# First head's stacks in three transfers by tokens, and values ahead of the spreading

## The chip, the cores and the metric

The kernel runs on one core of a Trainium2 chip. The metric is device time in microseconds, the median of several executions. One execution was also recorded by the hardware profiler; times inside it are counted from the start of its span. TensorE multiplies matrices, VectorE and ScalarE work elementwise, GpSimd does a few small operations, and SyncE issues every DMA of this kernel, in one queue.

## The reference

Two decoder layers over 1040 tokens (16 meta tokens and 1024 others) of width 1024, in float32. A layer computes

```
hn = rmsnorm(h, norm1_g)
q, k, v, u = split(hn @ w_in)
q, k = rope(q), rope(k)                       # 4 heads, two components of 64 each
lam = exp(sum(lam_q1*lam_k1)) - exp(sum(lam_q2*lam_k2)) + lam_init
a = softmax(q0 k0) - lam * softmax(q1 k1)     # causal
attn = rmsnorm(a @ v, subln_g) * (1 - lam_init)
conv = silu(layer_norm(depthwise(glu(u)), ...))
h = h + concat(attn, conv) @ w_out
h = h + (silu(gate) * up) @ w_down            # gate, up from rmsnorm(h, norm2_g)
```

and a last rmsnorm follows.

## The kernel before, in words

Activations lie transposed: channels on the 128 partitions, tokens along the rows. Each value that a matmul reads is split into a high and a low float32r part (`hh` and `hl` for the hidden state, two tiles for each weight), and a product takes three matmuls (high by high, high by low, low by high). Tokens are cut into three chunks, `CH0` = 0 to 272, 272 to 656, 656 to 1040.

The order on each engine is not that of the code. A scheduler of the tile framework simulates the program when it is built and fixes each engine's order and each tile's buffer. On the chip every engine then takes its own list strictly in turn. A row that waits holds up all behind it on its engine, and SyncE's list of DMAs is such a list. The DMAs count completion on eight semaphores in rotation, and a DMA that reuses one waits until the DMA eight places ahead has landed.

Layer 0 begins like this. While the input arrives, `project_qk` with `pre` multiplies the first two weight blocks of head 0 (accumulators `done`, L360): three chunks in PSUM tiles `pj` and three in `tr`. There are three `pj` buffers but only two `tr` buffers, so the third `tr` chunk (24 matmuls of 384 columns) needs one that has been copied out (L368). Beside it the squares of the hidden state are added up. `rsqrt_cols` sums them over the channels with one-column matmuls (L177) for nine blocks of tokens, VectorE scales (L179, L181), GpSimd takes the power -1/2 (L183). `spread` turns the nine columns into a row on all partitions: VectorE scales a diagonal (L198), TensorE multiplies by ones (L199), ScalarE copies out (L202). The tables of cosine and sine (L715) are multiplied by that row and used for the rope of q and k (L293), and the result is split into a pair of `ST` tiles (L285 on ScalarE for the high half, L286 on VectorE for the low half).

`make_stacks` then moves partitions with DMAs (L399): for each of the two components three tiles `S` of 128 rows, all from 32-row pieces of the `ST` pair. `small_params` loads the lambda parameters (L665) and reduces them to `nlam`. `project_v` makes the values chunk by chunk (L272, then ScalarE L428, a transpose L413 or L417, and ScalarE L414 or L420). `attention` takes query blocks of 16 and then eight times 128: `scores` (L455, L456, then VectorE and an exp on ScalarE, L466), the combination with `nlam` (L469 to L471), transposes (L483, L492) and values (L503). Between its steps the projection of the next head is woven in (`weave`). Weights come through `wsplit`: one DMA (L216), one ScalarE split (L222), one on VectorE (L223); `fetch` makes a block one ahead of the one asked for.

Of the kernel before, what the change touches and what calls it, by code (L numbers as in the profile page):

```python
# [10 lines left out]
F32 = mybir.dt.float32  # L11
F32R = mybir.dt.float32r
BF16 = mybir.dt.bfloat16
AF = mybir.ActivationFunctionType
# [5 lines left out]
L = 1040  # L20
D = 1024
KD = D // P
# [11 lines left out]
CH0 = ((0, 272), (272, 656), (656, 1040))  # L34
# [47 lines left out]
def tok(i):  # L82
    return (0, META) if i == 0 else (META + P * (i - 1), META + P * i)


def build(tc, xT, w_in, w_out, w_gu, w_down, params, lams, ctab, consts, tabs, outT):
    nc = tc.nc
    V, S, G, T_ = nc.vector, nc.scalar, nc.gpsimd, nc.tensor
# [12 lines left out]
    def nm(s):  # L101
        uid[0] += 1
        return f"{s}{uid[0]}"

    def big(dt=F32):
        return sp.tile([P, SW], dt, tag="S", name=nm("S"), bufs=SB)
# [11 lines left out]
    def tmp(dt=F32):  # L118
        return tp.tile([P, TW], dt, tag="T", name=nm("T"), bufs=TB)
# [15 lines left out]
    def small(n=NQ):  # L135
        return tp.tile([P, 16], F32, tag="small", name=nm("s"), bufs=16)

    def ps(tag):
        return pp.tile([P, 512], F32, tag=tag, name=nm(tag), bufs=PS_BUFS[tag])
# [29 lines left out]
    def rsqrt_cols(sq, n, blocks=range(NQ)):  # L169

        i0, i1 = blocks[0], blocks[-1] + 1
        pst = ps("sc")
        ms = small()
        V.memset(ms, 1.0)
        for i in blocks:
            a, b = tok(i)
            T_.matmul(pst[:b - a, i:i + 1], lhsT=sq[:, a:b], rhs=ones[:, 0:1], start=True, stop=True)  # L177
        f0 = max(i0, 1)
        V.tensor_scalar(ms[:, f0:i1], pst[:, f0:i1], 1.0 / n, EPS, op0=ALU.mult, op1=ALU.add)  # L179
        if i0 == 0:  # L180
            V.tensor_scalar(ms[:META, 0:1], pst[:META, 0:1], 1.0 / n, EPS, op0=ALU.mult, op1=ALU.add)  # L181
        rc = small()
        G.tensor_tensor(rc[:, i0:i1], ms[:, i0:i1], mhalf[:, i0:i1], op=ALU.pow)  # L183
        return rc

    def spread(rc, blocks=range(NQ), out=None):

        r = big() if out is None else out
        for k0, k1 in KCH:
            bl = [i for i in blocks if k0 <= tok(i)[0] < k1]  # L190
            if not bl:
                continue
            pb = ps("sc")
            dg = tmp()
            for i in bl:
                a, b = tok(i)
                n_ = b - a
                V.tensor_scalar(dg[:n_, a - k0:b - k0], ident[:n_, :n_], rc[:n_, i:i + 1], None, op0=ALU.mult)  # L198
                T_.matmul(pb[:, a - k0:b - k0], lhsT=ones[:n_, :], rhs=dg[:n_, a - k0:b - k0],  # L199
                          start=True, stop=True)  # L200
            lo, hi = tok(bl[0])[0], tok(bl[-1])[1]
            S.activation(r[:, lo:hi], pb[:, lo - k0:hi - k0], AF.Copy)  # L202
        return r
# [78 lines left out]
    hs = list(zip(hh, hl))  # L282

    def split(hi, lo, src):
        S.activation(hi, src, AF.Copy)  # L285
        V.tensor_tensor(lo, src, hi.bitcast(F32), op=ALU.subtract)  # L286
# [5 lines left out]
    def tt(o, a, b, op):  # L292
        V.tensor_tensor(o, a, b, op=op)  # L293
# [4 lines left out]
    def tick(c):  # L298

        credit[0] += c  # L300
        while credit[0] >= BGSTEP:
            credit[0] -= BGSTEP
            if bg:
                bg.pop(0)()
# [17 lines left out]
    def drain(*gens):  # L322
        for g in gens:
            for c in g:
                tick(c)
# [16 lines left out]
        return pads[which][turns[which] % 2]  # L342


    def project_qk(l, h, cosr, sinr, st, pre=None):
        if pre is None:
            wa = fetch("in", l, 3 * h)
            wb = fetch("in", l, 3 * h + 1)
        else:
            done = []  # L350
            for c0, c1 in CH0:
                done.append((ps("pj"), ps("tr")))
            lag = 2
            steps = [(i, k + lag * i) for i in range(2) for k in range(KD)]
            for i, k in sorted(steps, key=lambda t: (t[1], t[0])):
                k -= lag * i
                for q, (x, y) in enumerate(((0, 0), (0, 1), (1, 0))):
                    if True:
                        for c, (c0, c1) in enumerate(CH0):
                            T_.matmul(done[c][i][:, :c1 - c0], lhsT=pre[i][k][x],  # L360
                                      rhs=hs[k][y][:, c0:c1], start=(k == 0 and q == 0),
                                      stop=(k == KD - 1 and q == 2))
        st += [pair(F32R) for _ in range(2)]
        if pre is not None:
            ab = [big(), big()]
            for c, (c0, c1) in enumerate(CH0):
                for i in range(2):
                    S.activation(ab[i][:, c0:c1], done[c][i][:, :c1 - c0], AF.Copy)  # L368
        for c, (c0, c1) in enumerate(CH0):
            n = c1 - c0  # L370
            if pre is None:
                pa, pb = ps("pj"), ps("pj" if h else "tr")
                mm3(pa[:, :n], wa, hs, c0, c1)
            else:
                pa, pb = ab[0][:, c0:c1], ab[1][:, c0:c1]
            t = [tmp() for _ in range(4)]
            tt(t[0][:, :n], pa[:, :n], cosr[:, c0:c1], ALU.mult)
            tt(t[1][:, :n], pa[:, :n], sinr[:, c0:c1], ALU.mult)
            yield 10 * n
            if pre is None:  # L380
                mm3(pb[:, :n], wb, hs, c0, c1)
            tt(t[2][:, :n], pb[:, :n], sinr[:, c0:c1], ALU.mult)
            tt(t[3][:, :n], pb[:, :n], cosr[:, c0:c1], ALU.mult)
            tt(t[0][:, :n], t[0][:, :n], t[2][:, :n], ALU.subtract)
            tt(t[1][:, :n], t[1][:, :n], t[3][:, :n], ALU.add)
            for x in range(2):
                split(st[0][:, x, c0:c1], st[1][:, x, c0:c1], t[x][:, :n])
            yield 10 * n

    def make_stacks(st):  # L390
        stacks = []
        for c in range(2):
            q = slice(32 * c, 32 * c + 32)
            k = slice(64 + 32 * c, 96 + 32 * c)
            three = []
            for parts in (((0, q), (1, q)), ((0, k), (0, k)), ((1, k), (1, k))):
                s = big(F32R)
                for j, (x, rows) in enumerate(parts):
                    nc.sync.dma_start(s[64 * j:64 * j + 64, :L].bitcast(F32), st[x][rows].bitcast(F32))  # L399
                three.append(s)  # L400
            stacks.append(three)
        return stacks

    def project_v(l, h, rcol, out):
# [277 lines left out]
    for l in range(DEPTH):  # L682
# [9 lines left out]
        pre = None  # L692
        if l == 0:
            raws = []
            pre = []
            sqacc = big()
            for k in range(KD):
                if k in (0, 2):
                    pre.append(fetch("in", 0, k // 2))
                raw = big() if k else xraw  # L700
                raws.append(raw)
                if k:
                    nc.sync.dma_start(raw[:, :L], xT[k])
                gsplit(hh[k], hl[k], raw[:, :L], col("g1", 0, k))
                for c0, c1 in HALVES:
                    t = raw[:, c0:c1]
                    S.activation(sqacc[:, c0:c1] if k == 0 else t, t, AF.Square)
                    if k:
                        tt(sqacc[:, c0:c1], sqacc[:, c0:c1], t, ALU.add)
            nc.sync.dma_start(con, consts)  # L710
        rcol = rsqrt_cols(sqacc, D)
        rs = spread(rcol)
        cosr, sinr = big(), big()
        for t, i in ((cosr, 0), (sinr, 1)):
# [19 lines left out]
                if j in DVEJ:  # L734
                    conv_dve(l, j, zs[j][0], ys)

        st, vs = [], []
        drain(project_qk(l, 0, cosr, sinr, st, pre))
        if l == 0:
            for i in range(DEPTH):  # L740
                small_params(i)
        cats, fin = [], []
        for h in range(NH):
            stacks = make_stacks(st)
            vs = []
            drain(project_v(l, h, rcol, vs))
            if fin:
                finalize(*fin.pop())
            st = []
            if h + 2 == NH:  # L750
                fill, ratio = chain(project_qk(l, h + 1, cosr, sinr, st), glus((0,))), RA
            elif h + 1 < NH:
                fill, ratio = project_qk(l, h + 1, cosr, sinr, st), 1.3
            else:
                fill, ratio = glus((1, 2)), 1.8
            weave(attention(l, h, stacks, *vs, nlams[l], cats, fin), fill, ratio)
            drain(fill)
# [6 lines left out]
        for cat in cats:  # L764
            hi, lo = big(F32R), big(F32R)
            a = chunks[0][0]
# [118 lines left out]
        steps = [(j, q) for j in range(NF) for q in PRODS]  # L885
# [30 lines left out]
        for i, n in enumerate(OCN):  # L916
            w = fetch("oc", l, n)
            t = acc[n]
# [18 lines left out]
        for c, (s0, s1) in enumerate(sub):  # L937
            T_.matmul(sb[c][:, :s1 - s0], lhsT=xc["a11"][0][0][:, :P], rhs=xc["a11"][0][0][:, s0:s1],
                      start=True, stop=True)
# [67 lines left out]
        i = 0  # L1007
        for j in range(NF):
            gn = GROUPS[l][gi]
            m = len(mids)  # L1010
# [178 lines left out]
```

## Time and profile before

| | us |
|---|---|
| median of 3 runs (2387.89 to 2388.52) | 2388.34 |
| the profiled execution | 2387.03 |
| its span | 2385.3 |
| TensorE busy in the span | 2333.7 (98%) |
| VectorE busy | 1670.9 (70%) |
| ScalarE busy | 987.2 (41%) |

Busy time is an average over the whole span. The change concerns the first 80 us, and there the table of stretches tells more than the totals: busy time of each engine, the clock that TensorE was granted as a share of full speed, and what the DMA engines moved. The name behind an arrow in a row is what ended a wait.

### The profile page before, as it was taken

What the parts mean: (1) busy time and instruction counts of PE and PEld (TensorE: products, weight loads), DVE (VectorE), ACT (ScalarE), POOL (GpSimd) and SP (SyncE); (2) the same over time, 40 slices, a digit from 0 to 9 for tenths busy, and PEclk for the clock granted to TensorE, in tenths of its full rate; (3) what the DMA queues carried; (4) which work ended last, traced back from release to release, by engine and by line L of the source; (5) the groups of instructions that cost most, each with busy time, mean ns of one, the idle gap of its engine ahead of it and who ended that gap; (6) DMA issues with size and microseconds to landing.
All of it is one profiled execution on the core that took longest, in us unless ns stands there. A gap on an engine that the chain in (4) does not pass through costs nothing.

```text
span 2385.3 us, 36659 instructions
## 1 busy us (share of the span) xinstructions
PE 2333.7 (98%) x14407; PEld 2140.8 (90%) x14407; DVE 1670.9 (70%) x3476; ACT 987.2 (41%) x2074; POOL 33.8 (1%) x29
## 2 busy tenths in 40 slices
PE   8999999999999999999999999999999999999998
PEld 7899999989999999999999999987788888888887
DVE  7676799786656657566766768997856556556566
ACT  5565462553323223233535555536523223233242
POOL 0000000000000000000000000000000000000000
PEclk9999999999999999999999999999999999999999
DMA  4332422101112121111244314221121121111212
GB/s 163 94 76 68 121 66 61 49 29 60 46 45 64 35 63 40 59 56 43 90 128 102 74 44 112 76 54 45 36 62 55 43 62 39 59 59 39 60 56 71
DMA packets 84460, 155.29 MB, mean 65 GB/s; under 512 B 10048, under 2 KB 33600, under 8 KB 84288
## 3 DMA queue, kind: packets, MB, share of 16 engines
q1 hardware_dynamic: 84288, 152.95, 22.2%
q8 instruction: 114, 1.87, 0.3%
q14 instruction: 58, 0.48, 0.1%
HBM read 114.64 MB, written 8.45 MB: 52 GB/s over the span
## 4 chain that ended last, share of the span: by engine, by line
PE 86%; DVE 9%; ACT 2%; issue 1%; POOL 1%; DMA 1%; SPq 1%; DVEq 0%; POOLq 0%; ACTq 0%
PE pj L272 26%; PE sc L901 16%; PE pj L901 10%; PE tr L901 10%; PE sc L272 10%; DVE S L590 4%; PE tr L503 3%; PE tr L272 2%; PE sc L455 2%; PE tr L492 1%; PE sc L456 1%; PE sc L199 1%; DVE S L293 1%; DVE cw L610 1%; DVE S L286 1%
## 5 line engine op out<-in xcount | busy, mean ns | idle before, releaser
L272 PE MATMUL pj<-hh,w 128*128 128x384 f32 (+1 forms) x1776 | 342.5, 327 | 0.7 <-ACT S L368 0.7
L285 ACT ACTIVATE w<-w 128x512 fp32r<-128x512 f32 x308 | 187.0, 627 | 318.5 <-DVE w L293 242.9
L286 DVE TENSOR_TENSOR w<-w,w 128x512 fp32r<-128x512 f32 x308 | 209.5, 690 | 128.9 <-PE sc L901 53.8
L272 PE MATMUL pj<-S,w 128*128 128x384 f32 (+3 forms) x1164 | 296.2, 351 | 1.5 <-ACT S L285 0.9
L272 PEld LDWEIGHTS pj<-hh,w 128*128 128x128 f32 x1776 | 285.9, 189 | 2.7 <-ACT S L368 1.0
L901 PE MATMUL sc<-S,w 128*128 128x260 f32 (+1 forms) x1188 | 286.3, 322 | 0.0
L222 ACT ACTIVATE w<-w 128x512 fp32r<-128x512 f32 (+1 forms) x204 | 117.6, 577 | 308.3 <-DMA w<-in_w_down 167.9
L272 PEld LDWEIGHTS pj<-S,w 128*128 128x128 f32 x1164 | 204.4, 188 | 22.8 <-ACT S L285 1.9
L901 PEld LDWEIGHTS sc<-S,w 128*128 128x128 f32 x1188 | 198.6, 191 | 17.7
L272 PE MATMUL sc<-m,w 128*128 128x384 f32 (+3 forms) x804 | 211.5, 346 | 0.0
L272 PE MATMUL pj<-m,w 128*128 128x384 f32 (+3 forms) x804 | 211.4, 346 | 0.0
L901 PE MATMUL sc<-hh,w 128*128 128x260 f32 (+1 forms) x594 | 192.3, 324 | 6.9 <-ACT w L285 6.9
L901 PE MATMUL sc<-hl,w 128*128 128x260 f32 (+1 forms) x594 | 190.9, 321 | 0.0
L272 PE MATMUL pj<-hl,w 128*128 128x384 f32 (+1 forms) x888 | 174.4, 327 | 0.0
L223 DVE TENSOR_TENSOR w<-w,w 128x512 fp32r<-128x512 f32 (+1 forms) x204 | 127.1, 623 | 51.7 <-ACT w L222 45.2
L901 PE MATMUL tr<-S,w 128*128 128x260 f32 (+1 forms) x594 | 157.8, 320 | 3.1 <-ACT S L802 3.1
L901 PE MATMUL tr<-hl,w 128*128 128x260 f32 (+1 forms) x594 | 158.1, 320 | 0.0
L901 PE MATMUL pj<-S,w 128*128 128x260 f32 (+1 forms) x594 | 158.1, 320 | 0.0
L901 PE MATMUL pj<-hh,w 128*128 128x260 f32 (+1 forms) x594 | 157.7, 320 | 0.0
L272 PEld LDWEIGHTS sc<-m,w 128*128 128x128 f32 x804 | 143.1, 188 | 12.7
L272 PEld LDWEIGHTS pj<-m,w 128*128 128x128 f32 x804 | 143.1, 188 | 12.6
L590 DVE SCALAR_TENSOR_TENSOR S<-S,par,S 128x1037 f32<-128x1037 f32 (+15 forms) x120 | 153.2, 1278 | 0.6
(214 smaller groups left out, 4599.4 us busy)
## 6 DMA issues: line engine op xcount, KB each, us to landing
w<-in_w_gu SPq DMA_DIRECT2D x176, 256.0 KB, 3.0
S<-ST SPq DMA_DIRECT2D x96, 260.0 KB, 5.2
w<-in_w_in SPq DMA_DIRECT2D x80, 256.0 KB, 3.2
w<-in_w_down SPq DMA_DIRECT2D x96, 192.0 KB, 2.4
w<-in_w_out SPq DMA_DIRECT2D x32, 256.0 KB, 2.8
S<-in_xT SPq DMA_DIRECT2D x8, 520.0 KB, 7.3
w<-in_w_down SPq DMA_DIRECT2D x16, 256.0 KB, 2.7
S<-in_tabs SPq DMA_DIRECT2D x4, 520.0 KB, 5.4
```

Of the source, the lines that this page charges most:

```text
L199: T_.matmul(pb[:, a - k0:b - k0], lhsT=ones[:n_, :], rhs=dg[:n_, a - k0:b - k0], start=True, stop=True)
L222: S.activation(hi, rw, AF.Copy)
L223: V.tensor_tensor(lo, rw, hi.bitcast(F32), op=ALU.subtract)
L272: T_.matmul(out, lhsT=w[k][wi], rhs=xs[k][xi][:, c0:c1], start=(q == 0 and k == 0), stop=(q == 2 and k == n - 1))
L285: S.activation(hi, src, AF.Copy)
L286: V.tensor_tensor(lo, src, hi.bitcast(F32), op=ALU.subtract)
L293: V.tensor_tensor(o, a, b, op=op)
L455: T_.matmul(pc[:sz, :n], lhsT=qs[:, qa:qb], rhs=kk[:, k0:k1], start=True, stop=False)
L456: T_.matmul(pc[:sz, :n], lhsT=qs[:, qa:qb], rhs=kl[:, k0:k1], start=False, stop=True)
L503: T_.matmul(po[:sz, :P], lhsT=lh, rhs=rh, start=(j == 0), stop=(j == len(blocks) - 1))
L590: bg.append(lambda o=o: V.scalar_tensor_tensor(y[:, o:L], z[:, :L - o], cw(o), y[:, o:L], op0=ALU.mult, op1=ALU.add))
L901: T_.matmul(outs[c][:, :s1 - s0], lhsT=w[wi][:, k * P:(k + 1) * P], rhs=xc[q][k][xi][:, s0:s1], start=(first and p == 0 and k == 0), stop= ...
```

## The change

It does two things, for layer 0 and head 0 only. The first q/k products are a function of their own, `first_qk`, called ahead of `rsqrt_cols`, and it copies its accumulators out at once; the values' generator is made there too, and its first stretch (the 272-token chunk) is run between `rsqrt_cols` and `spread`. And the stacks are moved chunk by chunk: `project_qk` calls `make_stacks` after each chunk's split, with the six stack tiles made beforehand. A part of a stack is moved by DMAs of 32 rows and 272 or 384 columns, 24 for a chunk, 72 in all, where twelve of 64 rows and 1040 columns did it. Later heads and layer 1 go as before.

```diff
-    def project_qk(l, h, cosr, sinr, st, pre=None):
-        if pre is None:
+    def first_qk(pre):
+
+        done = []
+        for c0, c1 in CH0:
+            done.append((ps("pj"), ps("tr")))
...
+        ab = [big(), big()]
+        for c, (c0, c1) in enumerate(CH0):
+            for i in range(2):
+                S.activation(ab[i][:, c0:c1], done[c][i][:, :c1 - c0], AF.Copy)
+        return ab
+
+    def project_qk(l, h, cosr, sinr, st, ab=None, stacks=None):
+        if ab is None:
             wa = fetch("in", l, 3 * h)
             wb = fetch("in", l, 3 * h + 1)
...
             for x in range(2):
                 split(st[0][:, x, c0:c1], st[1][:, x, c0:c1], t[x][:, :n])
+            if stacks is not None:
+                make_stacks(st, c0, c1, stacks)
             yield 10 * n
 
-    def make_stacks(st):
-        stacks = []
+    def make_stacks(st, c0=0, c1=L, into=None):
+        stacks = into or []
...
-            for parts in (((0, q), (1, q)), ((0, k), (0, k)), ((1, k), (1, k))):
-                s = big(F32R)
+            for m, parts in enumerate((((0, q), (1, q)), ((0, k), (0, k)), ((1, k), (1, k)))):
+                s = into[c][m] if into else big(F32R)
                 for j, (x, rows) in enumerate(parts):
-                    nc.sync.dma_start(s[64 * j:64 * j + 64, :L].bitcast(F32), st[x][rows].bitcast(F32))
+                    if into is None:
+                        nc.sync.dma_start(s[64 * j:64 * j + 64, :L].bitcast(F32), st[x][rows].bitcast(F32))
+                        continue
+                    for i in range(2):
+                        a = 64 * j + 32 * i
+                        nc.sync.dma_start(s[a:a + 32, c0:c1].bitcast(F32), st[x][rows, i, c0:c1].bitcast(F32))
...
+        ab, stacks, vs = None, None, []
+        if l == 0:
+            ab = first_qk(pre)
         rcol = rsqrt_cols(sqacc, D)
+        first_v = project_v(l, 0, rcol, vs)
+        if l == 0:
+            tick(next(first_v))
         rs = spread(rcol)
...
-        st, vs = [], []
-        drain(project_qk(l, 0, cosr, sinr, st, pre))
+        st = []
+        if l == 0:
+            stacks = [[big(F32R) for _ in range(3)] for _ in range(2)]
+        drain(project_qk(l, 0, cosr, sinr, st, ab, stacks))
         if l == 0:
             for i in range(DEPTH):
                 small_params(i)
...
-            stacks = make_stacks(st)
-            vs = []
-            drain(project_v(l, h, rcol, vs))
+            if l or h:
+                stacks = make_stacks(st)
+            if h:
+                vs = []
+                drain(project_v(l, h, rcol, vs))
+            else:
+                drain(first_v)
```

What the scheduler makes of it shows in two places. The first is TensorE's order around the norm's sums in layer 0. The changed kernel's lines are numbered differently: its L356 is L360 of before, and the tile `sc` written by L177 holds the sums. Before:

```order
L360 MATMUL tr_278<-hl_94,w_146 128x272
L360 MATMUL tr_280<-hl_94,w_146 128x384
L177 MATMUL sc_223<-ones,S_125 16x1
L177 MATMUL sc_223<-ones,S_125 128x1 x4
L360 MATMUL tr_278<-hh_86,w_147 128x272
L360 MATMUL tr_280<-hh_86,w_147 128x384
L177 MATMUL sc_223<-ones,S_125 128x1 x4
L199 MATMUL sc_240<-T_241,ones 128x16
```

And in the changed kernel, at the same place, where `tr_228` is the third chunk, of which the first and the last two of 24 matmuls are shown, and `pj_410` the first stretch of values:

```order
L177 MATMUL sc_381<-ones,S_125 16x1
L177 MATMUL sc_381<-ones,S_125 128x1 x4
L272 MATMUL pj_410<-hh_79,w_164 128x272
L272 MATMUL pj_410<-hh_80,w_164 128x272
L272 MATMUL pj_410<-hh_81,w_164 128x272
L356 MATMUL tr_228<-hh_79,w_140 128x384
...
L356 MATMUL tr_228<-hl_94,w_146 128x384
L356 MATMUL tr_228<-hh_86,w_147 128x384
L177 MATMUL sc_381<-ones,S_125 128x1 x4
L272 MATMUL pj_410<-hh_82,w_164 128x272
```

The last four blocks' sums now stand behind three matmuls of values and the 24 of the third chunk, and the rest of the first stretch of values follows them, ahead of the spreading.

The second place is SyncE's queue around the stacks of head 0 (`S` from `ST`). Before, from the lambda loads on:

```order
L665 DMA T_479<-in_lams 128x256
L665 DMA T_487<-in_lams 128x256
L216 DMA w_656<-in_w_in 128x512
L399 DMA S_495<-ST_427 64x1x1040
L399 DMA S_495<-ST_428 64x1x1040
L399 DMA S_498<-ST_427 64x1x1040 x2
L399 DMA S_501<-ST_428 64x1x1040 x2
L399 DMA S_504<-ST_427 64x1x1040
L399 DMA S_504<-ST_428 64x1x1040
L399 DMA S_507<-ST_427 64x1x1040 x2
L399 DMA S_510<-ST_428 64x1x1040 x2
L216 DMA w_662<-in_w_in 128x512
```

In the changed kernel, with the first and the last rows of the 72 transfers:

```order
L730 DMA S_465<-in_tabs 128x1040
L730 DMA S_466<-in_tabs 128x1040
L216 DMA w_722<-in_w_in 128x512
L407 DMA S_475<-ST_481 32x272 x2
L407 DMA S_475<-ST_482 32x272 x2
...
L407 DMA S_479<-ST_481 32x384 x4
L407 DMA S_480<-ST_482 32x384 x4
L674 DMA T_597<-in_lams 128x256
L674 DMA T_605<-in_lams 128x256
L216 DMA w_728<-in_w_in 128x512
```

The lambda loads moved from ahead of the stacks to behind all of them, and a weight block (`w_716`, `w_722`) moved ahead. On ScalarE the split of `w_728` stands ahead of the first query block's exps. On TensorE the first two scores of the fourth query block stand ahead of 24 matmuls of the next head's projection, and the first block's transpose behind 20 of these.

## Rows read from the trace of the kernel before

**Rows 1.** Table of stretches, 25 to 95 us: busy time and instructions by engine, clock, DMA share, GB/s.

```profile
core 0: us, PE busy (x) PEld busy (x) DVE busy (x) ACT busy (x) POOL busy (x), PEclk, DMA share, GB/s
...
30.00:40.00 10.00, 6.76 (x39) 6.34 (x39) 4.45 (x17) 2.16 (x7) 1.80 (x1) 0.66 0.00 0
60.00:65.00 5.00, 4.53 (x28) 4.20 (x26) 0.32 (x2) 0.02 (x1) 0.00 (x0) 1.00 0.96 239
65.00:75.00 10.00, 5.65 (x25) 4.90 (x26) 3.12 (x19) 4.15 (x18) 0.00 (x0) 0.72 0.72 187
...
85.00:95.00 10.00, 10.00 (x68) 9.27 (x67) 8.86 (x34) 6.67 (x22) 0.00 (x0) 1.00 0.01 2
```

**Rows 2.** Waits of TensorE, 25 to 90 us: total, times, longest.

```profile
PE sc L199 <- DVE T L198: 2.5, 1, 2.5
PE sc L456 <- DMA S<-ST: 2.2, 1, 2.2
```

**Rows 3.** Instructions in order of time, SyncE's queue: start, duration, line, count.

```profile
49.78 2.16 SPq L665 DMA_DIRECT2D T<-in_lams  x2
...
52.63 13.17 SPq L399 DMA_DIRECT2D S<-ST  x12
65.90 3.61 SPq L216 DMA_DIRECT2D w<-in_w_in  x4
```

**Rows 4.** Instructions in order of time, all engines, 25 to 46 us.

```profile
30.95 0.95 PE L177 MATMUL sc<-ones,S 128*128 128x1 f32 x8
...
34.42 4.31 PE L199 MATMUL sc<-T,ones 16*128 16x16 f32 x18 [2.52 <-DVE T L198]
...
44.71 0.74 ACT L285 ACTIVATE ST<-T 128x272 fp32r<-128x272 f32 x2
45.16 0.79 DVE L286 TENSOR_TENSOR ST<-T,ST 128x272 fp32r<-128x272 f32 x2 [1.29 <-ACT ST L285]
```

**Rows 5.** The chain that ended last, in order of time, third chunk: start, duration.

```profile
40.10 4.20 PE tr L360 x24
```

**Rows 6.** One line's instructions, L199 in layer 1: durations in ns, first and last start.

```profile
L199 PE MATMUL sc<-T,ones x18: 257/275/278, 1217.8 to 1220.0; 128*128 128x128 f32 x16, 16*128 16x16 f32 x2
```

**Rows 7.** Instructions in order of time, SyncE's queue, start of the kernel and conv.

```profile
2.59 0.91 SPq L558 DMA_DIRECT2D ct<-in_ctab  x2
...
388.27 5.09 SPq L601 DMA_DIRECT2D S<-S  x8
```

**Rows 8.** DMA lines of SyncE: issue min/median/max in ns; landing of L601.

```profile
L601 SPq DMA_DIRECT2D S<-S x32: 571/597/1811, 352.0 to 1576.6; - x32
DMA to landing us min/median/max: 2.4/2.5/4.5
...
L399 SPq DMA_DIRECT2D S<-ST x12: 557/939/2090, 52.6 to 64.5; - x12
...
L216 SPq DMA_DIRECT2D w<-in_w_in x80: 327/328/2649, 1.6 to 1513.8; - x80
```

**Rows 9.** DMA issues by transfer: KB each, median us from issue to landing.

```profile
w<-in_w_in SPq DMA_DIRECT2D x80, 256.0 KB, 3.2
...
S<-in_tabs SPq DMA_DIRECT2D x4, 520.0 KB, 5.4
```

**Rows 10.** Instructions in order of time, all engines, 70 to 78 us, first query blocks.

```profile
70.46 0.49 PE L456 MATMUL sc<-S,S 128*16 128x16 f32 x2 [2.23 <-DMA S<-ST]
...
71.05 0.31 ACT L466 ACTIVATE p<-p,s 16x16 f32<-16x16 f32 x1 [3.65 <-DVE s L465]
...
71.36 0.61 ACT L222 ACTIVATE w<-w 128x512 fp32r<-128x512 f32 x1
...
72.61 0.22 DVE L471 SCALAR_TENSOR_TENSOR p<-p,s,p 16x16 f32<-16x16 f32 x1
...
74.34 0.19 PE L483 MATMUL tr<-con,p 16*16 16x16 f32 x1
...
77.61 0.27 PE L483 MATMUL tr<-con,p 128*16 128x128 f32 x1
```

More of the change, by code (lines that the diff above doesn't have):

```diff
@@ L342, in padded @@
         return pads[which][turns[which] % 2]
-    def project_qk(l, h, cosr, sinr, st, pre=None):
-        if pre is None:
+    def first_qk(pre):
+        done = []
+        for c0, c1 in CH0:
+            done.append((ps("pj"), ps("tr")))
+        lag = 2
+        steps = [(i, k + lag * i) for i in range(2) for k in range(KD)]
+        for i, k in sorted(steps, key=lambda t: (t[1], t[0])):
+            k -= lag * i
+            for q, (x, y) in enumerate(((0, 0), (0, 1), (1, 0))):
+                for c, (c0, c1) in enumerate(CH0):
+                    T_.matmul(done[c][i][:, :c1 - c0], lhsT=pre[i][k][x],
+                              rhs=hs[k][y][:, c0:c1], start=(k == 0 and q == 0),
+                              stop=(k == KD - 1 and q == 2))
+        ab = [big(), big()]
+        for c, (c0, c1) in enumerate(CH0):
+            for i in range(2):
[3 more added lines that the diff above has]
+        if ab is None:
             wa = fetch("in", l, 3 * h)
             wb = fetch("in", l, 3 * h + 1)
[L349 to L362, printed above, removed]
-        st += [pair(F32R) for _ in range(2)]
[L364 to L368, printed above, removed]
+        st += [pair(F32R) for _ in range(2)]
         for c, (c0, c1) in enumerate(CH0):
             n = c1 - c0
-            if pre is None:
+            if ab is None:
                 pa, pb = ps("pj"), ps("pj" if h else "tr")
@@ L379, in project_qk @@
             yield 10 * n
-            if pre is None:
+            if ab is None:
                 mm3(pb[:, :n], wb, hs, c0, c1)
@@ L395, in make_stacks @@
             three = []
-            for parts in (((0, q), (1, q)), ((0, k), (0, k)), ((1, k), (1, k))):
-                s = big(F32R)
+            for m, parts in enumerate((((0, q), (1, q)), ((0, k), (0, k)), ((1, k), (1, k)))):
+                s = into[c][m] if into else big(F32R)
                 for j, (x, rows) in enumerate(parts):
-                    nc.sync.dma_start(s[64 * j:64 * j + 64, :L].bitcast(F32), st[x][rows].bitcast(F32))
+                    if into is None:
[4 more added lines that the diff above has]
+                        nc.sync.dma_start(s[a:a + 32, c0:c1].bitcast(F32), st[x][rows, i, c0:c1].bitcast(F32))
                 three.append(s)
-            stacks.append(three)
+            if into is None:
+                stacks.append(three)
         return stacks
```

## The prediction

> **What bounds the kernel now.** I read the table of stretches first. TensorE is busy 10.00 of 10 us between 85 and 95 (and so it goes on), so a delay that reaches it there is not given back; it is idle for 3.24 us between 30 and 40 and for 4.35 us between 65 and 75, with a granted clock of 0.66 and 0.72 on average (its levels are 0.5 and 1.0 of full speed, 1.2 and 2.4 GHz) [rows 1]. Those two holes are all that the change can fill in this region: 7.6 us, and what the half clock costs. The waits of TensorE name the causes: 2.5 us for the spreading's VectorE scalings in the first hole, 2.2 us for the last stack transfers in the second [rows 2]. Then I followed SyncE's queue: two loads of lambda parameters from 49.78, twelve stack transfers that occupy the queue for 13.17 us from 52.63, weights behind them at 65.90 [rows 3].
>
> **The change part by part.** I place three events in the changed order and compare one position of TensorE: the transposes of the second query block, before at 77.61 [rows 10].
>
> *First hole.* The third q/k chunk (24 matmuls, 4.20 us [rows 5]) and the first stretch of values now stand ahead of the spreading. TensorE gets no more work. But the changed order also puts the last batch of the norm's sums (0.95 us, before from 30.95 to 31.90 [rows 4]) behind these 24 matmuls. They can start when ScalarE has copied the accumulator whose PSUM buffer they reuse; TensorE arrives there at about 31.05 by my estimate, since it saves the batch and gets three matmuls of values. 31.05 + 4.20 + 0.95 = 36.2: the pow on GpSimd, VectorE's scalings and all behind them start 4.3 us later than before. Something comes back: the spreading's 18 matmuls took from 34.42 to 38.73, 4.31 us, in the stretch of low clock [rows 1, 4]; in layer 1 the same 18 went from 1217.8 to about 1220.3, 2.5 us [rows 6]. That is 1.8, and the changed order takes some VectorE waiting out with it; I take 2.4 us later in all. The rope tables' loads stand behind a weight load that waits for the last matmul of the first two chunks, which stays near 29; with 5.4 us to land [rows 9] they arrive by 35 and are used near 41, so that move costs nothing, and each us beyond that slack would cost one.
>
> *First part of the stacks.* Before, the first chunk's high halves were written by 45.45 and the low ones by 45.95 [rows 4]. 2.4 us later, the first transfers (which need only the high halves) can go at about 47.6. Before, the first stack went at 52.63: 5.0 us are gained here.
>
> *The queue.* Twelve transfers become 72: 24 for each part, of 32 rows each. All 72 stand on SyncE ahead of both lambda loads, which before stood ahead of the stacks. The trace has no transfer of this shape. From below: plain loads from HBM take 0.327 us at least to issue [rows 8], with 0.05 between two 0.38; back to back they follow each other at 0.455 (two in 0.91 [rows 7]). From above: the conv's SBUF-to-SBUF transfers of 65 KB, eight in 5.09 us, 0.64 each [rows 7], of which the issue is 0.597, at least 0.571 [rows 8]. The old stacks took 0.557 at least, 0.939 in the median [rows 8]; the median is the engines' time for 260 KB, and the bytes in all are unchanged. I take 0.62, since the new ones are SBUF to SBUF too, as is each row with a least issue over 0.5. 72 x 0.62 = 44.6. The data are not late: the last chunk is split 2.4 us later than before, about 56, and is wanted at 47.6 + 48 x 0.62 = 77.
>
> By the Trainium skill (Perfetto Trace Analysis, section DMA Optimizations) splitting transfers may let some start sooner and so the whole end sooner, where the DMA engines are mostly idle. Here they moved 239 GB/s between 60 and 65 [rows 1], and what the split multiplies is the issue on one queue. The same skill (DMA: Bandwidth & Descriptors, section Issuing engines are not separate DMA queues) calls the time to initiate a DMA usually small beside the DMA itself. The conv's rows show 0.597 us of issue for 2.5 of landing [rows 8]; by the rule the queue would need little more than the bytes' 13.2 us, which is the third rival's case.
>
> *What waits for the queue.* The first query block needs lambda, now loaded at the queue's end: 47.6 + 44.6 = 92.2, and two plain issues (0.9) make 93.1. The weight load behind them counts as well, since the changed order puts its split on ScalarE ahead of the first block's exps: landing 3.2 [rows 9], split 0.61 [rows 10]. Before, from the second exp's start to the end of the subtraction it took 71.05 to 72.83 [rows 10]; now both exps lie there, 0.5 more, so 2.3. T = 93.1 + 3.2 + 0.6 + 2.3 = 99.2 for the first block's transpose, before at 74.34 [rows 10]. Lambda's own arithmetic hides beside that weight load. TensorE's order gives it nothing to do meanwhile: values, the next head's first projection chunk and 20 matmuls of its second run out by about 76, since the fourth block's first scores wait for 36 transfers: 47.6 + 22.3 + 2.5 = 72.4, later than the 70.46 at which scores resumed before [rows 10]. About 20 us of idle lie before that and 23 after it. The restart at a low clock I cost at nothing, since before had one too; it may cost 1.5 more.
>
> *The sum.* The second block's transpose came 3.27 us after the first [rows 10]; now T + 3.3 = 102.5. In the changed order 25 matmuls of 384 columns are still to do there that before were done: 25 x 0.175 (4.20 / 24) = 4.4. The delay is 102.5 + 4.4 - 77.6 = 29.3 us. From there both orders hold the same work and become the same within head 1, and TensorE stays full [rows 1]. The profiled execution took 2387.03 for a span of 2385.3; plus 29.3 that is 2416.3. The median of the runs shown is 1.3 above the profiled one, so I say 2417.
>
> **The rivals.** With y for one stack issue the delay is 72 y - 15.3.
>
> Second: the new transfers have plain patterns on both sides, so they cost what plain loads cost. For it: every row over 0.5 regroups partitions (64 or 128 rows from 32 or 16, or back), none of the new ones does. Against it: no SBUF-to-SBUF row is cheap. 0.455 gives +17.5, 2406; 0.38 gives +12.1, 2400.
>
> Third, the other side: the price goes with the rows. A quarter of the rows at a quarter of 0.327 is 0.08, with the gap 0.13, so the bytes decide, 13.2 us as before [rows 3]: 13.2 - 15.3 = -2.1 us, 2386. It decides below 0.21 an issue. Against it: in the program each transfer waits until the one eight places ahead has landed, and SBUF-to-SBUF landings take 2.4 at least [rows 8]; 2.4 / 8 = 0.30 would make it +6.3.
>
> Fourth: the queue costs what I say but half is given back, because the later blocks of head 0 find stacks, weights and lambda landed and TensorE's order waits less for VectorE. For it: VectorE was busy for only 3.12 of the ten us from 65 [rows 1]. Against it: TensorE is full after 85. 2403.
>
> That the first stretch of values doesn't fill the hole is no rival: it fills it, and the norm's chain is late for it.
>
> **How the numbers follow.** Forecast 0.64; plain price 0.18; price by rows 0.09; half given back 0.09. The likeliest gives 2417, its own range 2413 to 2423 (0.59 and 0.65 an issue, 1.5 us either way for the place of the first issue, the low clock). The range of eight in ten takes in half given back and the plain price at 0.455 and most of the way to 0.38: 2401 to 2423. About 0.2% (4.8 us) is what a measurement of this kernel can tell from no change. Slower by more: 0.64 + 0.18 + 0.09 = 0.91. The price by rows is split: same 0.06, and faster 0.03, if the holes close better than I reckon.
>
> **What would show it.** Right: SyncE issuing without a pause from about 47.6 until past 90, each stack transfer 0.55 to 0.62 us; the lambda loads behind; VectorE waiting for them longest of all it waits for early on; TensorE all but idle from about 76 to 99 at a low granted clock; the norm's last sums near 35 instead of 31. Wrong: issues below 0.25 us, lambda loads before 65, or TensorE busy in that stretch; then the second hole is closed and the kernel is no slower. If an issue costs 0.38 to 0.46, it is the price that fails, not the mechanism.

## The result, and the profile after

The changed kernel takes 2418.68 us (median of 4 runs, 2418.02 to 2419.91), the kernel before 2388.12 us on the same chip (4 runs). The ratio is 1.0129, with a 95% interval from 1.0117 to 1.0141: slower by 30.6 us, where 2417 had been forecast. The profiled execution took 2419.91 us for a span of 2418.1.

TensorE does no more work than before (14,407 matmuls, 2334.9 us busy against 2333.7). The table of stretches shows where it stands still; the columns are those of [rows 1].

```profile
30.00:40.00 10.00, 10.00 (x72) 9.70 (x71) 2.87 (x9) 3.15 (x8) 2.23 (x1) 1.00 0.45 158
...
50.00:60.00 10.00, 3.78 (x29) 3.40 (x27) 6.05 (x14) 3.26 (x8) 0.00 (x0) 0.92 0.20 54
60.00:65.00 5.00, 2.02 (x9) 1.75 (x10) 0.89 (x8) 0.00 (x0) 0.00 (x0) 0.50 0.24 61
65.00:75.00 10.00, 4.68 (x19) 3.92 (x19) 0.64 (x2) 1.14 (x4) 0.00 (x0) 0.50 0.30 77
75.00:85.00 10.00, 1.94 (x14) 1.72 (x13) 0.00 (x0) 0.00 (x0) 0.00 (x0) 0.84 0.30 76
85.00:95.00 10.00, 0.00 (x0) 0.00 (x0) 0.00 (x0) 0.00 (x0) 0.00 (x0) 0.50 0.33 84
95.00:105.00 10.00, 5.09 (x18) 4.22 (x19) 6.68 (x31) 4.88 (x21) 0.00 (x0) 0.50 0.34 106
105.00:115.00 10.00, 9.99 (x63) 9.31 (x62) 7.89 (x35) 6.73 (x23) 0.00 (x0) 0.94 0.04 17
115.00:125.00 10.00, 9.98 (x67) 9.16 (x66) 8.91 (x31) 6.43 (x21) 0.00 (x0) 1.00 0.01 2
```

The first hole of [rows 1] is filled: 10.00 of 10 us at full clock. In place of the second, between 65 and 75, there is one that begins near 53 and reaches to 100, with some work in it until 77. No engine works between 85 and 95, and the DMA engines stand at a third: what runs then is SyncE's queue, which comes next (start, duration, line, count; compare [rows 3]).

```profile
47.32 45.97 SPq L407 DMA_DIRECT2D S<-ST  x72
93.39 1.00 SPq L674 DMA_DIRECT2D T<-in_lams  x2
94.44 32.72 SPq L216 DMA_DIRECT2D w<-in_w_in  x6
```

72 transfers in 45.97 us are 0.638 us each, without a pause. The line's own durations (min, median, max in ns) and its time to landing:

```profile
L407 SPq DMA_DIRECT2D S<-ST x72: 517/588/663, 47.3 to 92.7; - x72
DMA to landing us min/median/max: 1.8/1.9/2.0
```

The longest waits of TensorE between 25 and 120 us, and of VectorE between 60 and 120 (total, times, longest):

```profile
PE tr L492 <- ACT p L475: 23.0, 1, 23.0
PE sc L464 <- DMA S<-ST: 8.9, 3, 5.2
PE sc L465 <- DMA S<-ST: 5.6, 3, 2.4
```

```profile
DVE T L293 <- DMA T<-in_lams: 22.1, 1, 22.1
```

The first view names ScalarE's exp as what TensorE waits for. ScalarE was not busy, however; the instructions in order of time show what it stood behind.

```profile
95.58 0.29 DVE L293 TENSOR_TENSOR T<-T 128x128 f32<-128x128 f32 x1 [22.13 <-DMA T<-in_lams]
...
97.65 0.63 ACT L222 ACTIVATE w<-w 128x512 fp32r<-128x512 f32 x1 [0.60 <-DMA w<-in_w_in]
98.19 0.29 ACT L475 ACTIVATE p<-p,s 16x16 f32<-16x16 f32 x1
...
99.91 0.18 PE L492 MATMUL tr<-con,p 16*16 16x16 f32 x1 [22.97 <-ACT p L475]
...
103.56 0.42 PE L492 MATMUL tr<-con,p 128*16 128x128 f32 x1
```

The lambda product (L293) starts when its load has landed, behind the 72 transfers; the weight's split (L222) starts 3.2 us after the weight's own issue; the exps (L475) stand behind the split in ScalarE's order. The last two rows answer to 74.34 and 77.61 of [rows 10].

### The profile page after: what moved, and what is told of

It is laid out like the page before. It is cut to its first block, busy times and chain, and to the rows that moved or that the text cites. A ratio compares the mean times of both kernels' runs of the same rounds, so it can differ in the third digit from the quotient of the medians.

```text
span 2418.1 us, 36756 instructions
## 1 busy us (share of the span) xinstructions
PE 2334.9 (97%) x14407; PEld 2142.6 (89%) x14407; DVE 1670.6 (69%) x3476; ACT 987.4 (41%) x2074; POOL 34.2 (1%) x29
## 4 chain that ended last, share of the span: by engine, by line
PE 84%; DVE 9%; ACT 2%; SPq 2%; issue 1%; POOL 1%; DMA 1%; DVEq 0%; POOLq 0%; ACTq 0%
PE pj L272 25%; PE sc L922 15%; PE tr L922 10%; PE pj L922 10%; PE sc L272 10%; DVE S L599 4%; PE tr L512 3%; PE tr L272 2%; SPq L407 2%; PE sc L464 1%; PE tr L501 1%; PE sc L465 1%; DVE S L293 1%; DVE cw L619 1%; DVE S L286 1%
## 5 line engine op out<-in xcount | busy, mean ns | idle before, releaser
L272 PE MATMUL pj<-hh,w 128*128 128x384 f32 (+1 forms) x1776 | 348.3, 330 | 0.0
L222 ACT ACTIVATE w<-w 128x512 fp32r<-128x512 f32 (+1 forms) x204 | 117.4, 576 | 307.9 <-DMA w<-in_w_down 156.8
```

Of the source, the lines that this page charges most:

```text
L222: S.activation(hi, rw, AF.Copy)
L272: T_.matmul(out, lhsT=w[k][wi], rhs=xs[k][xi][:, c0:c1], start=(q == 0 and k == 0), stop=(q == 2 and k == n - 1))
```

## The experiments

**The parts alone.** The token parts stay; the first q/k projection and the first values go back to their old places.

```diff
-        if l == 0:
-            ab = first_qk(pre)
         rcol = rsqrt_cols(sqacc, D)
-        first_v = project_v(l, 0, rcol, vs)
-        if l == 0:
-            tick(next(first_v))
         rs = spread(rcol)
...
+            ab = first_qk(pre)
             stacks = [[big(F32R) for _ in range(3)] for _ in range(2)]
```

> Token parts of the stacks alone: the first q/k products and the values stand where they stood before the change, the 72 transfers stay. Queue theory (lambda and weight loads wait behind 72 issues of 0.64 us): the queue starts 2.2 us earlier, at about 45.2, the lambda loads go out near 91, the first block's transpose comes near 97 to 101, and the time is 2414 to 2420 us, since TensorE idles in that stretch whether or not the first hole is filled. Rival (the norm's chain, moved behind the third chunk, is what costs): the loss goes with the move, 2388 to 2395.

Measured: 2420.65 us, ratio 1.0138 (1.0124 to 1.0151). The norm's last sums are at 31.63 again, the hole for the spreading is back, and the loss is still there in full: SyncE's queue is as in the changed kernel.

```profile
47.41 47.09 SPq L407 DMA_DIRECT2D S<-ST  x72
94.60 1.00 SPq L674 DMA_DIRECT2D T<-in_lams  x2
```

So the parts make the loss, not the norm's chain. The first transfer goes at 47.41 with the norm's sums early (expected: 45.2), and at 47.32 with them late: the early sums buy nothing here, where TensorE is granted a clock of 0.67 from 30 to 40 and of 0.82 from 40 to 50; in the changed kernel it is 1.00 in both.

**The move alone.** The first q/k and values stay early, the stacks are twelve whole transfers again.

```diff
-        if l == 0:
-            stacks = [[big(F32R) for _ in range(3)] for _ in range(2)]
         drain(project_qk(l, 0, cosr, sinr, st, ab, stacks))
...
-            if l or h:
-                stacks = make_stacks(st)
+            stacks = make_stacks(st)
```

> The move of the first q/k products and of the values' first stretch alone, with the stacks in twelve whole transfers as before the change. Queue theory: lambda loads are ahead of the stacks again, so the loss of 30 us is gone; the stacks start 2.6 us later than before (near 55.3) and scores resume near 73 instead of 70.5, but some 6 us more of the next head's projection is done by then: 2383 to 2388 us. Rival (the norm's chain): 2400 or more.

Measured: 2388.07 us, ratio 1.0000 (0.9992 to 1.0009). Both holes of [rows 1] are gone: 10.00 of 10 us are busy from 30 to 40 and from 65 to 75. The time is not better, since TensorE is idle elsewhere. One row of the table of stretches (here TensorE alone: time, busy, clock, DMA share, GB/s) of the kernel before, then of this one:

```profile
115.00:125.00 10.00, 9.99 (x66) 1.00 0.93 219
```

```profile
115.00:125.00 10.00, 5.57 (x39) 0.92 0.87 228
125.00:135.00 10.00, 10.00 (x56) 0.74 0.06 20
```

And the instructions there:

```profile
119.52 0.17 DVE L293 TENSOR_TENSOR s<-s,s 128x9 f32<-128x9 f32 x1 [1.94 <-POOL s L544]
...
119.93 1.64 DVE L557 TENSOR_SCALAR S<-S,s 128x128 f32<-128x128 f32 x8
...
121.69 0.16 DVE L474 TENSOR_REDUCE s<-p 16x1 f32<-16x16 f32 x1
```

```profile
121.88 0.31 ACT L475 ACTIVATE p<-p,s 16x16 f32<-16x16 f32 x1 [4.13 <-DVE s L474]
122.09 0.18 ACT L475 ACTIVATION_READ_ACCUMULATOR p<-p,s 16x1 f32 x1
122.18 2.12 ACT L429 ACTIVATE S<-tr,s 128x128 f32<-128x128 f32 x8
```

```profile
122.83 0.55 PE L426 MATMUL tr<-con,T 128*128 128x128 f32 x3 [4.22 <-ACT S L429]
```

At the first head's end VectorE waits 1.94 us for a power on GpSimd (L544) and then scales the head's output (L557). The second head's first reduction (L474) stands behind that, its exp (L475) behind the reduction, the copies of the values' transposes (L429) behind the exp, and TensorE behind the copies. The chain goes through the orders of four engines, and TensorE waits 4.2 us at its end. From 30 to 125 us TensorE gains 1.0 us of work in all (87.91 us busy against 86.93); the profiled spans (2386.2 and 2385.3) do not show that gain. The half clock after the new idle time and a start that was 0.5 us behind work against it, but the 0.9 us between the spans is no more than executions of one kernel differ by.

**Lambda loads early.** The changed kernel with the two lambda loads and their arithmetic ahead of the norm.

```diff
+        if l == 0:
+            for i in range(DEPTH):
+                small_params(i)
         rcol = rsqrt_cols(sqacc, D)
...
-        if l == 0:
-            for i in range(DEPTH):
-                small_params(i)
```

> The changed kernel with the lambda parameters loaded and reduced ahead of the norm's sums, so that their two loads stand ahead of the 72 transfers; the rest as in the change. Queue theory: the first block no longer waits for the queue's end, the wait left is for the parts themselves (second part's last piece near 80, third part's near 95, which the seventh query block needs): 2390 to 2400 us, most of the loss gone. Rival (the parts' own late landing is the cost, lambda only happened to be last): 2408 or more.

Measured: 2390.48 us, ratio 1.0012 (1.0003 to 1.0022). 28 of the 30.6 us are gone, although the 72 transfers take their 47.33 us as before. TensorE's waits between 45 and 130 us:

```profile
PE tr L426 <- ACT S L429: 2.9, 1, 2.9
PE sc L464 <- DMA S<-ST: 2.1, 3, 1.0
...
PE sc L465 <- DMA S<-ST: 0.9, 2, 0.5
```

The first block's transpose is at 67.08 here:

```profile
67.08 0.18 PE L492 MATMUL tr<-con,p 16*16 16x16 f32 x1
```

The 72 issues thus cost little by themselves: 3.0 us of waiting for stacks. What cost 28 us is the first block's small load behind them. The edit changes TensorE's order too: in the changed kernel the scores stand one behind another until 72 us and wait 14.5 us for stacks at the same pace of the queue; here the scheduler has put projection work between them. So the 28 us are the load's place together with the order that comes of it.

**Half as many transfers.** Each part's two 32-row transfers become one of 64 rows; the lambda loads stay behind.

```diff
-                    for i in range(2):
-                        a = 64 * j + 32 * i
-                        nc.sync.dma_start(s[a:a + 32, c0:c1].bitcast(F32), st[x][rows, i, c0:c1].bitcast(F32))
+                    nc.sync.dma_start(s[64 * j:64 * j + 64, c0:c1].bitcast(F32),
+                                      st[x][rows, :, c0:c1].bitcast(F32))
```

> The changed kernel with each piece moved as one transfer of 64 rows instead of two of 32: 36 transfers on the queue, the same bytes, lambda loads still behind them. Queue theory with a price per issue: 36 x 0.64 = 23 us, lambda near 71, the first block's transpose near 77: about 8 us slower than before, 2394 to 2399 us. Rival (a price by rows or bytes): halving the number changes nothing, 2415 to 2420.

Measured: 2397.89 us, ratio 1.0043 (1.0029 to 1.0056), 20.8 us below the changed kernel for 36 transfers less, 0.58 us each. Twice the bytes a transfer leave the issue where it was:

```profile
47.87 23.16 SPq L405 DMA_DIRECT2D S<-ST  x36
71.13 1.04 SPq L673 DMA_DIRECT2D T<-in_lams  x2
```

```profile
L405 SPq DMA_DIRECT2D S<-ST x36: 543/597/683, 47.9 to 70.4; - x36
```

The first block's transpose is at 77.76 here, 22.2 us earlier than in the changed kernel.

**Both remedies.** 64-row transfers and the lambda loads early, the last two edits together.

> The changed kernel with both remedies at once: 36 transfers of 64 rows, and the two lambda loads issued ahead of them. Theory A (what counts is what stands in SP's queue): the transfers take 36 x 0.643 = 23.2 us instead of 46, the first part is in its stacks near 56 and the third near 72 instead of 95, and the waits that the lambda kernel still has between 50 and 105 us (8.1 us of idle TensorE by its windows) mostly go: 2381 to 2386 us. Rival B (read from the kernel with the move alone: the work that TensorE can do without the stacks is a fixed stock, and what fills a hole early is missing at the end of the first head, where its transposes wait 4.2 us for ScalarE near 118 us): the time stays near the kernel before, 2386 to 2390.

Measured: 2380.47 us, ratio 0.9971 (0.9960 to 0.9981), 7 us faster than the kernel before. TensorE waits 1.4 us for stacks:

```profile
PE sc L463 <- DMA S<-ST: 0.7, 1, 0.7
PE sc L464 <- DMA S<-ST: 0.7, 1, 0.7
```

```profile
62.09 0.19 PE L491 MATMUL tr<-con,p 16*16 16x16 f32 x1
```

From 30 to 125 us it is idle for 2.0 us (kernel before: 8.1). Rival B falls: the holes filled early do not all come back at the head's end. The first block's transpose is at 62.09, where it was at 74.34 in [rows 10] and at 78.92 with the move alone. No run has these parts with a short queue and without the move, so how much of the 7 us is the parts' and how much the move's is not shown. My reading, which no run isolates either, is that with whole stacks the free projection work is used up before attention can start, and is missing at the head's end; with parts, attention starts 12 us earlier and the free work lasts through the head.

**Sums first.** As the last one, with the norm's sums ahead of the third q/k chunk.

```diff
-        if l == 0:
-            ab = first_qk(pre)
...
         rcol = rsqrt_cols(sqacc, D)
+        if l == 0:
+            ab = first_qk(pre)
```

> As the kernel with both remedies, and the sums of the first norm are issued ahead of the third q/k chunk instead of behind it, so that the norm's chain starts 4 us earlier. Theory A: a little faster still than with both remedies, by 1 to 4 us, 2379 to 2385. Rival B (the stock of free work decides): the same as with both remedies within 1 us. A third way: the sums wait for VectorE's squares as they do in the kernel before (1.9 us there), and the hole before the spreading opens again: 1 to 3 us slower than with both remedies.

Measured: 2379.36 us, ratio 0.9966 (0.9954 to 0.9979): 1.1 us below the last, too little to tell the two apart. The norm's sums are read at 33.32 instead of 37.53, and yet the first stack goes at 48.14 instead of 48.52: the spreading's matmuls stand in TensorE's order behind the first stretch of values, and start at 40.15.

```profile
40.15 0.39 PE L199 MATMUL sc<-T,ones 16*128 16x16 f32 x2
```

**The kernel before with early lambda loads.** The same move as above, on the kernel before and alone.

> The kernel before with one edit: the two lambda loads are issued ahead of the twelve whole stack transfers, and nothing else. Theory A (SP's queue): the loads' 2.16 us leave the queue's path, the stacks land some 2.2 us earlier, and the waits for them between 60 and 75 us shrink by as much: 2384 to 2387. Rival B: what is gained there comes back as a wait at the head's end, 2387 to 2389. Either way it bounds what the order of the lambda loads is worth without the parts.

Measured: 2389.78 us, ratio 1.0011 (1.0002 to 1.0020): slower, if by little, and not as theory A would have it. The loads had gone to 2.6 us, where the DMA engines are full. I took the start for the cause (TensorE's first product at 7.43 instead of 6.67 us). The rows show more: after the hole before the spreading the third q/k chunk runs at half clock until about 44.6 (0.77 on average from 40 to 50), its matmuls in pairs of 0.84 us first and 0.51 later.

```profile
43.03 0.84 PE L360 MATMUL tr<-hh,w 128*128 128x384 f32 x2
...
44.82 0.51 PE L360 MATMUL tr<-hh,w 128*128 128x384 f32 x2
```

ScalarE's copy of it, on which the stacks hang, is at 47.28, against 44.32 in the kernel before: about 1.1 us of the 3.0 were there already when the spreading began (35.55 against 34.42). The half clock does not need this edit: the kernel with the parts alone, whose lambda loads stand at the queue's end, starts its spreading at 35.09 and then has a granted clock of 0.82 from 40 to 50.

**The move alone with early lambda loads.**

> The move alone (first q/k and first values' stretch early, twelve whole transfers), and the two lambda loads ahead of these. Theory A: the transfers start 2.2 us earlier than in the kernel with the move alone, 2384 to 2387. Rival B: its holes at 30 and 60 us are filled already, its idle time stands near 118 us behind the head's tail, and nothing changes: 2387 to 2389.

Measured: 2386.59 us, ratio 0.9996 (0.9987 to 1.0005), not to be told from the kernel before. TensorE is again short of work at the head's end (7.41 of 10 us busy from 115 to 125). So the move gains nothing measurable with whole stacks, with the lambda loads in either place.

**Late lambda loads.** As the kernel with sums first, with the lambda loads just ahead of the stacks instead of at 2.6 us.

```diff
+        if l == 0:
+            for i in range(DEPTH):
+                small_params(i)
         st = []
         if l == 0:
             stacks = [[big(F32R) for _ in range(3)] for _ in range(2)]
```

> The kernel with 64-row parts and the sums first, with the two lambda loads between the tables and the first stack transfer, near 30 to 46 us, where the DMA engines stand at 0.02 to 0.49, instead of at 2.6 us, where they stand at 1.0. Theory C (the early place cost the start: the first product came at 7.2 to 7.4 us there, at 6.67 in the kernel before, and TensorE did 15.8 us of work in the first 25 against 17.8): 1 to 2 us faster than the same kernel with the early loads, 2377.5 to 2379. Rival (the start varies with the DMA engines from run to run and has nothing to do with the loads): the same, 2378.5 to 2380.5.

Measured: 2380.51 us, ratio 0.9971 (0.9961 to 0.9981). No gain, and the first product comes at 7.7 us without a lambda load before it. Theory C falls: the start varies by itself.

**The kernel before with late lambda loads.** The same place, on the kernel before.

> The kernel before with the two lambda loads between the tables and the twelve whole transfers, and nothing else; with the loads at 2.6 us the same edit took 2389.8. Theory C: the start is that of the kernel before, first product near 6.7 us, and the queue is rid of 2.2 us: 2384.5 to 2387. Rival (the start varies by itself, and what the queue gains comes back in the wait for the stacks or at the head's end): 2387 to 2390.

Measured: 2390.54 us, ratio 1.0013 (1.0004 to 1.0022), on the rival's side and a little beyond it. The rows show a third cause, which I had not thought of. With its loads, lambda's arithmetic came forward, into the rope's work on VectorE:

```profile
44.34 0.49 ACT L368 ACTIVATE S<-tr 128x384 f32<-128x384 f32 x1 [3.51 <-PE tr L360]
44.73 0.20 ACT L670 ACTIVATE s<-s 128x2 f32<-128x2 f32 x1
```

```profile
44.95 0.16 DVE L672 SCALAR_TENSOR_TENSOR nlam<-s 128x1 f32<-128x1 f32 x1 [2.18 <-ACT s L670]
```

```profile
54.68 13.56 SPq L399 DMA_DIRECT2D S<-ST  x12
```

VectorE waits 2.18 us for lambda's exp, which ScalarE reaches only behind the copy of the last q/k accumulator. The rope is late by that, and the twelve transfers start 2.05 us later than in [rows 3]: as much as the queue had gained. With the loads at 2.6 us that wait is not there; that kernel lost its time in other places, its later start and the half clock of its third chunk. What brings that half clock on stays open.

**Two parts.** As the kernel with late loads, the second and third part joined (768 tokens).

```diff
-            if stacks is not None:
-                make_stacks(st, c0, c1, stacks)
+            if stacks is not None and c != 1:
+                make_stacks(st, c0 if c == 0 else CH0[1][0], c1, stacks)
```

> As the kernel with the late lambda loads, with two parts (272 tokens, then 768) instead of three: 24 transfers, the last part at 0.75 to 1.0 us each as it carries twice the bytes. Issue theory: the first part is in its stacks as before, the second ends 4 to 6 us earlier than the third did; since the kernel with three parts waits for its stacks only 1.4 us in all, it gains at most that: 2376.5 to 2379. Rival: the second chunk's blocks now wait for the whole 768 tokens, and TensorE is short of work between 60 and 66 us: 1 to 3 us slower than with three parts, 2379 to 2382.

Measured: 2380.31 us, ratio 0.9970 (0.9960 to 0.9980): the same as three parts. The last transfer's issue ends at 66.43 instead of 72.87, 6.4 us earlier, and buys nothing, since TensorE no longer waits there.

```profile
48.42 7.73 SPq L405 DMA_DIRECT2D S<-ST  x12
...
56.88 9.55 SPq L405 DMA_DIRECT2D S<-ST  x12
```

**The changed kernel with late lambda loads.**

> The changed kernel with nothing else edited than the place of the two lambda loads: between the tables and the 72 transfers. Theory A (all of the loss is that the loads and the weight after them stand behind 72 issues; the weight still does): without the start's 2 us that the loads at 2.6 us cost, 2387 to 2390, so no loss against the kernel before and no gain. Rival (the weight w behind the 72, needed for the second head's projection, holds TensorE by itself): 2392 to 2400.

Measured: 2393.20 us, ratio 1.0020 (1.0010 to 1.0030). Theory A said 2390 at most, so its size is missed by 3 us; the rival's range holds the number, but not its reason, since TensorE waits for no weight between 45 and 130 us. It waits for stacks, 5.7 us against 3.0 with the loads at 2.6 us:

```profile
PE sc L464 <- DMA S<-ST: 3.5, 3, 1.6
...
PE sc L465 <- DMA S<-ST: 2.2, 2, 1.6
```

## Why the prediction was right

The mechanism was the forecast one, and each step can be set beside its row.

- *The first hole* fills, and the norm's last sums end at 36.63 (forecast 36.2). The spreading's 18 matmuls take 2.56 us there, from 39.66 to 42.22 (L199, x2 and x16), against the 2.5 of [rows 6].
- *The first part* goes at 47.32 (47.6).
- *The queue* takes 0.638 us a transfer; I had 0.62. Over 72 that is 1.3 us, and lambda's issues and the gap before them another 0.2; its loads end their issue at 94.39 (93.1). The cheaper prices of the rivals fall: the least of the 72 is 0.517. So SBUF-to-SBUF transfers were the right neighbours, though these regroup no partitions.
- *T*, the first block's transpose, is at 99.91 (99.2), behind lambda, the weight and its split in that order. Two errors partly cancel in it: the queue ended 1.3 us later than forecast, and from the split's end to T it took 1.6 us instead of 2.3. That the lambda loads behind the 72 carry nearly all of the loss is shown by moving them; the price of an issue by halving the transfers. The two together leave none of it.
- *The second block* comes 3.65 us after the first (3.3), at a granted clock of 0.50.
- *The idle time* before 77 was given as about 20 us and is 14.5 from 50 on: TensorE did its work there at a granted clock of 0.50 from 60 to 75, and so was busy for longer. The sum does not use this term.
- *The sum.* At the position I compared, the delay is 103.56 + 4.4 - 77.61 = 30.4 us (29.3). The low clock at the restart, which I had costed at nothing, adds little: further on, in the third head, the same transposes (L492 of before, L501 of the changed kernel) stand at 203.64 and 234.45, 30.8 us apart. The profiled executions differ by 32.9, and the rest comes much later, in work that the change does not touch. At the spreading of layer 1 the delay is 1249.67 - 1217.75 = 31.9. Between 1572 and 1577 the changed kernel's execution is granted a clock of 0.68, where that of the kernel before has 1.00 (1540 to 1545), and the delay grows from 32.0 to 33.3. Why the clock fell in one execution alone is not shown. The medians differ by 30.6. The forecast added the 1.3 us by which the median of before lay above its profiled execution; for the changed kernel the median lies 1.2 below. That 2417 came within 2 us of 2418.68 is therefore in part luck: several terms missed by about a microsecond, in both directions.
- *Half given back* falls: TensorE is busy for 9.98 us and more of every ten from 105 to 145, as it was in [rows 1], and the delay is still 30.8 us in the third head.

On the two rules weighed: the end of the stacks did not come sooner for being split, and the time to initiate was not small beside the transfer here, with 0.588 us of issue for 1.9 of landing, 72 times on one queue. For this shape the measurement decides, against what the Trainium skill (DMA: Bandwidth & Descriptors, section Issuing engines are not separate DMA queues) calls usual. What the Trainium skill (Perfetto Trace Analysis, section DMA Optimizations) says of splitting is not refuted as such. With 36 transfers and nothing urgent behind them attention starts 12 us earlier and the kernel, which has the move too, ends 7 us sooner, although the last transfer's issue ends at 72.41 instead of 65.80.

What I had not seen is that the change holds a gain at all. I priced the holes at 7.6 us and took them for lost; the parts with a short queue, together with the move, win about 7 us back.

## What to carry to other kernels

Before a transfer is split, count the issues, multiply by the issue time of the nearest row of the same kind, and read the queue's order for what stands behind them: here a load that takes a microsecond cost 25 to 28 us because 72 issues stood ahead of it. A hole that is filled with work from elsewhere is only a gain if that work is not what covers a later wait; look at where the borrowed work stood. And when a load is moved, its arithmetic moves with it and can block an in-order engine that the load never touched.

## What the runs showed of the hardware

- The issue of an SBUF-to-SBUF transfer hardly depends on its rows here: 0.588 us in the median for 32 rows, 0.597 for 64 rows of the same length. Longer rows cost more: with two parts, the twelve of 64 rows and 768 columns followed each other at 0.80 (9.55 us), and the 260 KB transfers of [rows 8] took 0.939.
- The landing is short for them: 1.8 to 2.0 us for 32 rows in the changed kernel, 2.1 to 2.5 for 64 in the kernel with half as many; in other runs single ones of these shapes took up to 3.9. One queue that issues without a pause kept the 16 DMA engines at only 0.30 to 0.33 of their time, 76 to 84 GB/s; with 64 rows a transfer they stood at 0.59 and 152 GB/s between 60 and 65 us.
- The start varies by about a microsecond from execution to execution: TensorE's first product came at 6.67 to 7.89 us, and these two ends are the kernel before and the kernel with the parts alone, which issue the same loads in the same order up to there.
